# Output stage of a hybrid decoder layer: two kinds of GpSimd sums held at their source place, and a wider spread of one product's weight splits

## The chip, the cores and the metric

One core of a Trainium2 chip runs the whole kernel in one launch. The metric is the device time of an execution in microseconds (us). The engines are TensorE (PE in the profile, with its weight loads as PEld), VectorE (DVE), ScalarE (ACT), GpSimd (POOL) and SyncE (SP), which here only issues DMA transfers.

## What is computed

One decoder layer, for a prompt of 2048 tokens and for 32 sample tokens, in float32. A projection of the normalised input gives four groups of columns: a convolution module, a pooling mixer, a stick-breaking attention and a cross-attention. Each result is multiplied by its gate; the four are concatenated to a row of 2048 and multiplied by `w_out` (2048 x 1024), normalised, added to the input and normalised again. The output stage, on which the change bears, is the last line but one:

```python
mix = jnp.concatenate([y_c * jax.nn.silu(cg), y_p * jax.nn.silu(pg),
                       y_s * jax.nn.silu(sg), y_m * jax.nn.silu(mg)], axis=-1)
out = rms_norm(mix @ w_out, post_g)
return x + out, conv_new, pool_new, k, v
...
y_prompt = rms_norm(xp, final_g)
```

## The kernel before

**The stages.** Input projection and sample attention fill the first 1700 us, prompt attention runs to about 1947 us, and the output stage runs from there to the end, with the last steps of the convolution module (`conv_post`) spread through it.

**The output product in seven.** `mix @ w_out` is cut two by two by two (pairs of token tiles, halves of the 2048, halves of the 1024 columns) and computed from seven block products instead of eight, numbered 1 to 7. Sums and differences of blocks of `mix` and of `w_out` replace the missing product. `weight_sums` made the sums of `w_out` earlier and left them in DRAM (`wsd`). The sums of `mix` are made in this stage by `out_combine`:

- Product 7: POOL subtracts two row blocks (L1702) and SP stores the difference to `msd` for product 6.
- Product 6: DVE subtracts that difference from another block (L1705); the result is the product's own operand. POOL then subtracts it from the rows that product 2 used (L1706), and SP stores this to `msd` (L1617) for product 3. So nothing in product 6 waits for L1706 itself; product 3 does, much later, and SP does at once, since the store stands in its queue.
- Product 5: POOL adds two row blocks (L1699). Both come with the load of product 4 (L1672), so the sum can run as soon as that transfer has landed. Its result is product 5's operand.

**Parts.** A product's work on one pair of token tiles is split into two halves of the contraction. Such a *part* `(product, i, half)` is four quarters, and a quarter is three matmuls against 512 columns: float32 is carried as a rounded high part and a rest, so high times high, rest of the weights times high, high times rest. There are 120 parts in a fixed list: product 1, product 7, then 2 and 6 in alternation, then 4, 5 and 3 in alternation. `i = 8` is the sample tokens. I number parts from 0; part 34 is (2,0,0), parts 38 and 39 are (6,0,0) and (6,0,1), parts 64 to 67 the last of product 6, part 69 is (4,0,1), part 72 the first of product 5.

**What a part needs.** The high and low part of its operand: `out_high`, a cast on ACT (L1714), then `out_low`, a subtraction on DVE (L1725). And four of the eight weight blocks of its product: `weight_high` on ACT (L1621, `wohi`) and `weight_low` on DVE (L1626, `wolo`), from a raw block that SP loads (L1599, L1602 or L1611). The first half of a product uses blocks 0 to 3, the second half blocks 4 to 7, one block per quarter.

**Order.** PE follows the order of the source (`manual_schedule`). On the other engines a planner orders the instructions when the program is built, by its own estimate of when each is ready, and an engine then works its queue strictly in order. So there are two places of an instruction: where the source traces it, and where the planner puts it. `tc.keep_in_program_order(ins)` ties the two a little: `ins` may not be issued ahead of the one instruction that was traced just before it on the same engine. It adds no wait for a result, and later instructions may still go ahead of it. L1621, L1626 and L1705 are held so already.

**Who traces what when.** The main loop walks the parts. After each quarter it advances the convolution by a step whenever a counter, raised by 1 per quarter, passes 0.9 (`OPACE`), then calls `weights_step(n + k / 4)`, which traces the weight steps due by then. `spread(gen, start, step)` makes step `k` of a product's weights due at part `start + step * k`. For product 6 the start is part 31, and block `j` is split in step `3 + j`. At the end of a part, `prepare` loads operands six parts ahead, combines four ahead and casts three ahead. One round of the convolution (`center`, `scale`, `point`) handles 256 tokens: PE sums squares (`cv`, L1460), ACT takes a root (L1461), DVE the reciprocal (L1462), then for two pairs of channel blocks DVE scales (L1469), ACT takes the sigmoid (L1472), DVE multiplies (L1476), ACT casts (L1478), DVE subtracts (L1481); the matmuls `cz` (L1502) of the pointwise layer follow, in four pieces, and DVE empties each from PSUM (L1505). The `cz` pieces share two PSUM buffers.

**Last steps.** `out_factor` (L1788, POOL) multiplies a stored half of the output, `oh`, by a gain, and `out_tile` normalises and stores a token tile. Blocks of `mix` are held in few buffers (`raw`: 4 of two blocks each; `wr`: 2 for weights).

Of the kernel before, what the change touches and what calls it, by code (L numbers as in the profile page):

```python
# [13 lines left out]
ALU = mybir.AluOpType  # L14
# [73 lines left out]
def kernel(  # L88
# [9 lines left out]
    pe, act, dve, pool, sp = nc.tensor, nc.scalar, nc.vector, nc.gpsimd, nc.sync  # L98
# [1492 lines left out]
    def weight_load(prod, j, raw):  # L1591

        if (prod, j) in seconds:
            return [seconds.pop((prod, j))]
        n, h = SUMS.get(prod, (0, 0))
        if raw == "opm":
            t = opm.tile([P, 512], F32, tag="raw", name=f"wor{prod}_{j}", bufs=3)
            if prod in SUMS:
                sp.dma_start(t, wsd[n, j, :, h])  # L1599
            else:  # L1600
                q = FACTORS[prod]
                sp.dma_start(t, w_out0[half_rows(j)[q // 10 - 1], 512 * (q % 10 - 1) : 512 * (q % 10)])  # L1602
            return [t]
        slot = (opx if raw == "wx" else op).tile([P, 2, 512], F32, tag=raw, name=f"wor{prod}_{j}",
                                                 bufs={"raw": RAWS, "wr": 2, "wx": 3}[raw])
        if prod in SUMS:
            two = wsd[n, j : j + 2, :, h]
        else:
            k = 4 + j if j < 4 else j - 4
            two = w_out0.rearrange("(b p) n -> b p n", p=P)[k : k + 2, :, :512]  # L1610
        sp.dma_start(slot, two.rearrange("b p n -> p b n"))  # L1611
        seconds[prod, j + 1] = slot[:, 1]
        return [slot[:, 0]]

    def store(key=None):
        while len(stores) > 2 or key in [k for k, *_ in stores]:
            sp.dma_start(*stores.pop(0)[1:])  # L1617

    def weight_high(prod, j, ts, pool_):
        hi, lo = [pool_.tile([P, 512], F32R, tag=f"wo{n}{j}", name=f"wo{n}{prod}_{j}", bufs=1) for n in ("hi", "lo")]  # L1620
        tc.keep_in_program_order(act.copy(hi, ts[0]))  # L1621
        ts += [hi, lo]

    def weight_low(prod, j, ts, eng):
        raw_, hi, lo = ts
        tc.keep_in_program_order(eng.tensor_tensor(out=lo, in0=raw_, in1=hi.bitcast(F32), op=ALU.subtract))  # L1626
        W[prod, j] = hi, lo

    def out_weights(prod, pool_, eng, lead=1, raw=lambda j: "opm", lag=1):


        ts = {}
        for j in range(lead):
            if j:
                yield
            ts[j] = weight_load(prod, j, raw(j))
        for j in range(8 + lag):
            yield
            if 0 < j < 9:
                weight_high(prod, j - 1, ts[j - 1], pool_)  # L1640
            if j >= lag:
                weight_low(prod, j - lag, ts.pop(j - lag), eng)
            if j < 8:
                store()
            if j + lead < 8:
                ts[j + lead] = weight_load(prod, j + lead, raw(j + lead))
# [47 lines left out]
    def out_combine(x):  # L1694
        prod, i, h = x
        store()
        ts = raws[x]
        if prod == 5 and i < LAST:
            pool.tensor_tensor(out=ts[1], in0=ts[0], in1=ts[1], op=ALU.add)  # L1699
            ts = ts[1:]  # L1700
        elif prod == 7:
            pool.tensor_tensor(out=ts[0], in0=ts[0], in1=ts[1], op=ALU.subtract)  # L1702
            stores.append(((0, i, h), msd[0, i, h], ts[0]))
        elif prod == 6:
            tc.keep_in_program_order(dve.tensor_tensor(out=ts[0], in0=ts[0], in1=ts[1], op=ALU.subtract))  # L1705
            pool.tensor_tensor(out=ts[2], in0=ts[2], in1=ts[0], op=ALU.subtract)  # L1706
            stores.append(((1, i, h), msd[1, i, h], ts[2]))
        raws[x] = ts[0]

# [217 lines left out]
    def side_work():  # L1927
        nonlocal opm, conv
        with tc.tile_pool(name="sm", bufs=1, side="left", reuse_waits="tile") as sm2:
            yield from sample_end(sm2, side_ps, S)  # L1930
        with tc.tile_pool(name="wsp", bufs=1, side="left", reuse_waits="tile") as wsp:
            yield from weight_sums(wsp)
        opm = ox.enter_context(tc.tile_pool(name="opm", bufs=1, side="left", reuse_waits="tile"))
        yield from out_weights(1, opm, pool)
        while (3, 0) not in flags:
            yield
        for x in lead_:
            out_load(x)
            out_combine(x)
            out_high(x)  # L1940
            out_low(x, pool)
            yield

        while (3, 1) not in flags:
            yield
        for x in parts[2 * LEAD : 2 * LEAD + 3]:
            out_load(x)
        cp = cx.enter_context(tc.tile_pool(name="cp", bufs=1, side="left", reuse_waits="tile"))
        conv = conv_post(cp, lambda n: conv_ps[0](n), lambda: cx.enter_context(
            tc.tile_pool(name="cpw", bufs=1, side="left", reuse_waits="tile")))  # L1950
        while "centered" not in flags:
            next(conv)
            yield
# [55 lines left out]
    op = oy.enter_context(tc.tile_pool(name="op", bufs=1, side="right", reuse_waits="tile"))  # L2009
# [9 lines left out]
    def weights_after():  # L2019


        at = parts.index

        def spread(gen, start, step):
            yield start
            for k, _ in enumerate(gen):
                yield start + step * k

        yield 2 * LEAD
        wr = lambda j: "wr"  # L2030
        yield from spread(out_weights(7, op, dve, 2, wr), 2 * LEAD, 1.5)
        yield from spread(out_weights(2, opm, dve, 2, wr), at((7, 0, 0)) + 1, 1.4)

        def place():

            nonlocal op2, opx, accp2
            yield at((2, 7, 0)) - 6
            for _ in conv:
                pass
            cx.close()  # L2040
            accp2 = oy.enter_context(tc.tile_pool(name="ops2", bufs=1, space=PSUM, side="right", reuse_waits="tile"))
            op2 = cx.enter_context(tc.tile_pool(name="op2", bufs=1, side="left", reuse_waits="tile"))
            opx = x6.enter_context(tc.tile_pool(name="opx", bufs=1, side="left", reuse_waits="tile"))

        def fourth():
            yield at((2, 7, 0)) - 5
            yield from spread(out_weights(4, op2, dve, 2, lambda j: "wx"), at((2, 7, 0)) - 4, 1)

        some = ("opm", "wr", "wr", "raw", "raw", "opm", "wr", "wr")
        yield from heapq.merge(spread(out_weights(6, op, dve, 3, lambda j: some[j]), at((2, 0, 0)) - 3, 0.55), place(),  # L2050
                               fourth(), spread(out_weights(5, opm, dve, 2, wr), at((2, 8, 0)) - 1, 1),
                               spread(out_weights(3, op, dve, 2, lambda j: "opm"), last_ + 1, 1))

    wts, wait = weights_after(), 0

    def weights_step(n):
# [11 lines left out]
    def prepare(n):  # L2068
        for d, f in ((3, out_load), (1, out_combine), (0, out_high)):
            for x in parts[: n + d]:  # L2070
                if x in ready[d]:
                    continue
                prod, i, h = x
                if d == 3 and not h and prod == 2:
                    while i < LAST and ("conv", i) not in flags:
                        next(conv, None)
                    if i == LAST:
                        for _ in conv:
                            pass
                f(x)  # L2080
                ready[d].add(x)
# [67 lines left out]
```

## Time and profile before

| | us |
|---|---|
| Runs of the kernel (3): median, lowest, highest | 2359.39, 2356.07, 2364.3 |
| The profiled execution: its own time | 2357.87 |
| Its span, from first to last instruction | 2356.2 |
| PE busy in the span | 2268.6 |
| DVE busy | 1718.0 |
| POOL busy | 1280.6 |
| Last matmul of part 119 begins | 2339 |

All times of the trace are counted from the span's start. The profiled execution lies 1.5 us below the median of the runs. In a row of the timeline stand the start, the time taken, the engine, the line, the operation, what it writes and reads, how many instructions the row merges, and in brackets how long the engine stood idle before it and what ended that. `SPq` is SP's queue: the row's time is the issue of the transfer, not the transfer.

### The profile page before, as it was taken

How to read it: one execution, taken by the hardware profiler on the slowest of the kernel's cores; microseconds unless marked ns; L12 is line 12 of the kernel's file. 1: busy time of each engine (PE TensorE's matmuls, PEld its weight loads, DVE VectorE, ACT ScalarE, POOL GpSimd, SP SyncE). 2: the span in 40 equal slices, each digit the busy share in tenths (PEclk: the TensorE clock that was granted, in tenths of full speed). 3: DMA queues.
4: the chain of work that ended last, by engine and by line, in shares of the span. 5: the costliest groups of instructions: out<-in, count | busy, mean ns of one | idle time of the engine just before them, and what ended most of it. 6: DMA issues, size and time to landing. Idle time of an engine off the chain costs nothing. (4 is left out here: it accounts for less than half of the span.)

```text
span 2356.2 us, 42223 instructions
## 1 busy us (share of the span) xinstructions
PE 2268.6 (96%) x16024; PEld 1767.5 (75%) x16024; DVE 1718.0 (73%) x2428; ACT 1118.3 (47%) x1947; POOL 1280.6 (54%) x1322
## 2 busy tenths in 40 slices
PE   7999999999999999999999999899999999999897
PEld 7998888888888777777777777555555557878775
DVE  5342786969647664577787868888897966787897
ACT  5322343342442322234242324788989875454554
POOL 3554545555464656545546463688988854432330
PEclk9999999999999999999999999999999999999999
DMA  6689977878678899987877884756544207866674
GB/s 212 196 283 298 343 267 257 288 248 289 243 262 314 311 352 338 322 287 260 304 264 257 280 273 143 176 170 165 161 131 117 77 23 225 283 223 215 208 247 159
DMA packets 336870, 557.94 MB, mean 237 GB/s; under 512 B 27986, under 2 KB 212434, under 8 KB 320267
## 3 DMA queue, kind: packets, MB, share of 16 engines
q1 hardware_dynamic: 281290, 286.53, 39.4%
q0 software_dynamic: 55376, 268.72, 32.0%
q8 instruction: 126, 2.06, 0.4%
q14 instruction: 78, 0.63, 0.1%
HBM read 465.09 MB, written 90.68 MB: 236 GB/s over the span
## 5 line engine op out<-in xcount | busy, mean ns | idle before, releaser
L966 DVE STREAM_TRANSPOSE T<-kt 128x1024 f32<-128x1024 f32 x256 | 308.6, 1225 | 182.8 <-PE sSA L979 170.0
L933 POOL DMA_INDIRECT vt<-in_cache_v_dram,idv x256 | 252.8, 988 | 255.5 <-PE sO L1018 194.9
L618 DVE SCALAR_TENSOR_TENSOR cacc<-U,par,cacc 128x512 f32<-128x512 f32 x480 | 359.7, 749 | 11.0
L1344 POOL TENSOR_TENSOR be<-be,E 128x512 f32<-128x512 f32 (+3 forms) x316 | 300.6, 967 | 60.4 <-DVE E L1335 26.6
L1335 DVE TENSOR_TENSOR_SCAN E<-gam,cr,ZM 128x513 f32<-128x513 f32 x192 | 232.7, 1262 | 14.1 <-ACT gam L1266 10.7
L933 POOL DMA_INDIRECT kt<-in_cache_k_dram,idk x128 | 128.3, 1002 | 198.8 <-DVE T L966 157.4
L1355 PEld LDWEIGHTS AT<-ident,be 128*128 128x128 f32 x1082 | 116.1, 141 | 128.0 <-ACT at L1361 48.2
L1969 PE MATMUL acc<-wohi,mh 128*128 128x512 f32 (+1 forms) x480 | 193.5, 403 | 1.9 <-ACT mh L1714 1.9
L1266 ACT ACTIVATE gam<-S,nbias_bc 128x1024 f32<-128x1024 f32 (+1 forms) x158 | 173.1, 1095 | 42.6 <-ACT be L1267 18.5
L1969 PE MATMUL acc<-wolo,mh 128*128 128x512 f32 (+1 forms) x480 | 189.5, 395 | 2.6 <-DVE wolo L1626 2.6
L1969 PE MATMUL acc<-wohi,ml 128*128 128x512 f32 x448 | 177.4, 396 | 5.6 <-DVE ml L1725 5.6
L1262 PE MATMUL S<-kT,Q 128*128 128x512 f32 (+1 forms) x632 | 174.6, 399 | 5.4 <-ACT be L1267 5.4
L1267 ACT ACTIVATE be<-S,bias_bc 128x1024 f32<-128x1024 f32 (+1 forms) x158 | 172.0, 1089 | 1.4 <-DMA gsd<-sg1sg 1.4
L1355 PE MATMUL AT<-ident,be 128*128 128x128 f32 x1082 | 157.3, 283 | 14.0 <-DVE at L1359 7.4
L1371 PE MATMUL av<-at,V 128*64 128x512 f32 (+3 forms) x640 | 152.2, 554 | 3.5 <-DVE sbo L1376 3.5
L979 PE MATMUL sSA<-T,W 128*32 128x128 f32 x4096 | 138.3, 276 | 1.8 <-DVE T L966 1.4
L979 PEld LDWEIGHTS sSA<-T,W 128*32 128x32 f32 x4096 | 104.6, 109 | 36.6 <-issue 29.1
L1018 PE MATMUL sO<-vt,saT 128*32 128x512 f32 x1024 | 122.3, 592 | 0.0
L1725 DVE TENSOR_TENSOR ml<-mr,mh 128x512 fp32r<-128x512 f32 x108 | 95.7, 897 | 35.0 <-ACT mh L1714 33.5
L1262 PEld LDWEIGHTS S<-kT,Q 128*128 128x128 f32 x632 | 105.0, 193 | 19.2 <-ACT be L1267 6.8
L1361 ACT COPY at<-AT 128x512 f32<-128x512 f32 x192 | 111.3, 679 | 12.2 <-PE AT L1355 12.2
L1332 DVE TENSOR_TENSOR_SCAN E<-gam,ZM 128x384 f32<-128x384 f32 (+1 forms) x124 | 94.3, 809 | 28.8 <-ACT gam L1266 22.0
(577 smaller groups left out, 6024.7 us busy)
## 6 DMA issues: line engine op xcount, KB each, us to landing
Q<-qd SPq DMA_DIRECT2D x64, 256.0 KB
mr<-mixd SPq DMA_DIRECT2D x32, 512.0 KB
mr<-mixd SPq DMA_DIRECT2D x48, 256.0 KB
xtp<-in_x_prompt_dram SPq DMA_DIRECT2D x16, 512.0 KB
kT<-kd SPq DMA_DIRECT2D x64, 128.0 KB
ws<-in_w_out_dram SPq DMA_DIRECT2D x16, 512.0 KB
wsd<-ws SPq DMA_DIRECT2D x16, 512.0 KB
msd<-mr SPq DMA_DIRECT2D x32, 256.0 KB
```

The lines of the kernel that those rows point to most:

```text
L618: dve.scalar_tensor_tensor(out=ps, in0=U[:, a + k : a + k + H], scalar=wd[:, k : k + 1], in1=ps, op0=ALU.mult, op1=ALU.add)
L933: pool.indirect_dma_start(out=dst, out_offset=None, in_=rows, in_offset=bass.IndirectOffsetOnAxis(ap=idx, axis=0))
L966: S["turn"] = dve.transpose(T[:, 2 * hh : 2 * hh + 2].rearrange("p s j t -> p (s j t)"), kt[:, 2 * hh : 2 * hh + 2].rearrange("p s j d -> ...
L979: pe.matmul(sSs[n][32 * g : 32 * g + 32, P * ml : P * (ml + 1)], lhsT=W[:, jj, :], rhs=T[:, :, jj, :], start=i == 0, stop=i == 3, tile_pos ...
L1262: pe.matmul(S[:, j, :w], lhsT=Q[:, x, P * (q2 + j) : P * (q2 + j + 1)], rhs=kt[:, :w], start=x == 0, stop=x == 1)
L1266: act.activation(out=ga, in_=S[:, :, :w], func=AF.Sigmoid, bias=nbias_bc[:, h : h + 1], scale=-1.0)
L1267: act.activation(out=be, in_=S[:, :, :w], func=AF.Sigmoid, bias=bias_bc[:, h : h + 1])
L1335: dve.tensor_tensor_scan(out=E[:, j][:, ::-1], data0=g_[:, j][:, ::-1], data1=ZM[:, 0:1].to_broadcast([P, 513]), initial=carry[hh, q2][:, ...
L1344: newest.append(pool.tensor_tensor(out=be[:, j, :m], in0=be[:, j, :m], in1=E[:, j, 513 - w : 513 - w + m], op=ALU.mult).ins)
L1355: pe.transpose(ap_[:, P * qt : P * (qt + 1)], A[hp, qb, kc, hh, qt][:, P * r : P * (r + 1)], ident)
L1371: pe.matmul(av[64 * hh : 64 * hh + 64, c], lhsT=V[:, 4 * kc + r, 64 * hh : 64 * hh + 64], rhs=ats.pop((hp, qb, kc, r, hh))[:, c], start=dg ...
L1969: pe.matmul(o[:rows], lhsT=m[a][:, k, :rows], rhs=W[prod, 4 * h + k][w], start=not cont and h == k == n == 0, stop=h == 1 and k == 3 and n ...
```

## The change

Two calls on POOL, L1699 and L1706, are wrapped in `tc.keep_in_program_order`, as the DVE call beside them already was. And the weight steps of product 6 are due every 0.7 parts instead of every 0.55: block `j` is split at part `31 + 0.7 * (3 + j)`, so block 0 at 33.1 instead of 32.65 and block 7 at 38.0 instead of 36.5. No instruction is added, removed or resized.

```diff
@@ out_combine
         if prod == 5 and i < LAST:
-            pool.tensor_tensor(out=ts[1], in0=ts[0], in1=ts[1], op=ALU.add)
+            tc.keep_in_program_order(pool.tensor_tensor(out=ts[1], in0=ts[0], in1=ts[1], op=ALU.add))
             ts = ts[1:]
...
             tc.keep_in_program_order(dve.tensor_tensor(out=ts[0], in0=ts[0], in1=ts[1], op=ALU.subtract))
-            pool.tensor_tensor(out=ts[2], in0=ts[2], in1=ts[0], op=ALU.subtract)
+            tc.keep_in_program_order(pool.tensor_tensor(out=ts[2], in0=ts[2], in1=ts[0], op=ALU.subtract))
@@ weights_after
-        yield from heapq.merge(spread(out_weights(6, op, dve, 3, lambda j: some[j]), at((2, 0, 0)) - 3, 0.55), place(),
+        yield from heapq.merge(spread(out_weights(6, op, dve, 3, lambda j: some[j]), at((2, 0, 0)) - 3, 0.7), place(),
                                fourth(), spread(out_weights(5, opm, dve, 2, wr), at((2, 8, 0)) - 1, 1),
```

## Prediction

> **What bounds the kernel now.** I read the page first, then the table by stretches (length, busy PE, PEld, DVE, ACT and POOL with counts, TensorE's clock, DMA), then the waits of TensorE in the output stage (total, times, longest), then the timelines around each wait.
>
> ```profile
> span 2356.2 us, 42223 instructions
> PE 2268.6 (96%) x16024; PEld 1767.5 (75%) x16024; DVE 1718.0 (73%) x2428; ACT 1118.3 (47%) x1947; POOL 1280.6 (54%) x1322
> ```
> ```profile
> 2050.00:2100.00 50.00, 45.70 (x231) 38.88 (x230) 43.64 (x73) 26.00 (x53) 16.05 (x15) 0.96 0.71 225
> 2200.00:2250.00 50.00, 47.16 (x205) 37.91 (x204) 44.83 (x77) 26.99 (x67) 8.21 (x6) 1.00 0.68 226
> ```
> ```profile
> PE acc L1969 <- DVE ml L1725: 5.6, 4, 3.5
> PE cz L1502 <- DVE cgt L1505: 4.3, 1, 4.3
> PE cz L1502 <- ACT shi L1478: 2.9, 2, 2.3
> PE acc L1969 <- DVE wolo L1626: 2.6, 1, 2.6
> PE acc L1969 <- ACT mh L1714: 1.9, 2, 1.2
> PE cz L1502 <- DVE slo L1481: 1.2, 2, 0.8
> ```
>
> TensorE is busy 96% of the span, and its order is fixed, so the change can act only through these waits (1930 us to the end): 18.5 us in 12 waits. POOL never ends one directly. DVE is the near second: 43.64 and 44.83 of 50 us. So the gain can hardly pass 18.5 us, and a change that delays one high or low part by more than its slack costs exactly that on the path.
>
> The edits do three things. They have TensorE wait less for `cgt` (term B), they make the last weight block of product 6 late (term C), and they let a POOL difference out sooner (term A).
>
> **Term B: fewer splits ahead of the pointwise layer's emptying.** VectorE and TensorE around the 4.3 us wait:
>
> ```profile
> 2064.87 0.68 DVE L1626 TENSOR_TENSOR wolo<-wor,wohi 128x512 fp32r<-128x512 f32 x1
> ...
> 2072.74 0.69 DVE L1626 TENSOR_TENSOR wolo<-wor,wohi 128x512 fp32r<-128x512 f32 x1
> ...
> 2074.50 4.05 DVE L1626 TENSOR_TENSOR wolo<-wor,wohi 128x512 fp32r<-128x512 f32 x3
> ...
> 2079.61 1.21 DVE L1626 TENSOR_TENSOR wolo<-wor,wohi 128x512 fp32r<-128x512 f32 x1
> 2080.74 0.47 DVE L1505 SCALAR_TENSOR_TENSOR cgt<-cz,par,cgt 128x256 f32<-128x256 f32 x1
> ```
> ```profile
> 2081.26 0.39 PE L1502 MATMUL cz<-shi,pwhi 128*128 128x256 f32 x1 [4.30 <-DVE cgt L1505]
> ```
>
> The third `cz` piece needs the PSUM buffer of the first, and L1505 stands behind a run of L1626. Six of product 6's splits lie before it: one at 2064.87 and the five from 2072.74 to 2079.61. Its own source place is the last quarter of part 35. By the new steps block 4 is due at part 35.9 and block 5 at 36.6, both behind it; four splits stay ahead. So L1505 moves forward by two L1626: 1.21 (row 2079.61) and 4.05 / 3 = 1.35, together 2.6 us. Bounds: 1.2 if the planner moves only one out of the way, 4.3 if the whole wait goes. I take −2.6, since DVE runs without a gap there.
>
> **Term C: the last split of product 6 becomes late.** Block 7's step is due at part 36.5 before and 38.0 after. Because `weight_high` and `weight_low` are held behind the instruction traced just before them, what matters is which one that is. Counting the convolution's steps (one per 0.9 quarter) from the `cv` matmul that the trace shows in the third quarter of part 37, two steps fall into the first quarter of part 38, and they end with the second pair of L1469 and L1472 of that round. Block 7 is traced right behind. So on ACT its cast cannot pass L1472's second pair, and on DVE its subtraction cannot pass L1469's. Now it follows L1505's third piece, far earlier. The round in the trace of before:
>
> ```profile
> 2088.51 0.59 PE L1460 MATMUL cv<-csq,ones_ln 128*128 128x256 f32 x2
> ...
> 2094.96 0.40 PE L1969 MATMUL acc<-wohi,mh 128*128 128x512 f32 x1
> 2095.20 0.39 PE L1969 MATMUL acc<-wolo,mh 128*128 128x512 f32 x1
> ```
> ```profile
> 2089.14 0.45 ACT L1461 ACTIVATE cv<-cv,eps_t 128x256 f32<-128x256 f32 x1 [0.62 <-PE cv L1460]
> ...
> 2098.05 0.84 ACT L1472 ACTIVATE csg<-ct,par 128x256 f32<-128x256 f32 x2 [1.01 <-DVE ct L1469]
> ```
> ```profile
> 2091.05 1.76 DVE L1462 RECIPROCAL cv<-cv 128x256 f32<-128x256 f32 x1
> 2092.71 0.67 DVE L1725 TENSOR_TENSOR ml<-mr,mh 128x512 fp32r<-128x512 f32 x1
> ```
> ```profile
> 2058.60 0.59 PE L1460 MATMUL cv<-csq,ones_ln 128*128 128x256 f32 x2
> ```
> ```profile
> 2069.89 0.84 ACT L1472 ACTIVATE csg<-ct,par 128x256 f32<-128x256 f32 x2 [0.70 <-DVE ct L1469]
> ```
>
> The chain from `cv` (2088.51) to the end of L1472's second pair (2098.89) is 10.4 us. A cast L1621 adds about 0.5 and a split L1626 about 0.7: the low part is there 11.6 us after `cv`. TensorE reaches the fourth quarter of part 39, block 7's first use, at 2094.96 and needs the low part at 2095.20, 6.7 us after `cv`. Both ends hang on the same `cv`, so an earlier or later TensorE does not help: a wait of 11.6 − 6.7 = 4.9 us, where there is none now. Lower bound: L1462 could start at 2089.6 (root done) instead of 2091.05 and the L1725 between could step back, 2.0 less, so 2.9. Upper: block 6's split now falls between L1462 and L1469 (0.7 to 1.2 more), so 6.1. I take +4.9. Behind the waiting cast on ACT stand the squares L1452 and casts L1714; nothing of these is due before TensorE itself moves on. Block 6 is held only behind L1461 and L1462 and comes in time: 2092.8 + 0.7, against its use a quarter ahead of 2094.96.
>
> The weight steps also move their transfers on SP:
>
> ```profile
> 2078.58 0.32 SPq L1681 DMA_DIRECT2D mr<-mixd  x1
> ...
> 2100.43 0.45 SPq L1611 DMA_DIRECT2D wor<-wsd  x1
> ```
>
> The first takes the buffer of blocks 3 and 4 the moment the last of the three L1626 ends, at 2078.55; with block 4 behind L1505's second piece it leaves some 3 us later, for part 41, which starts near 2098 and after term C near 2103: nothing. The second, a weight of product 5, takes the buffer of blocks 6 and 7, free at 2085.9 now and near 2097.5 then: still before 2100.43, nothing. Should either cover fail, the rows behind it on SP are late by the excess.
>
> On TensorE's clock after such a pause: the stretch 2050 to 2100 with the 4.3 us wait shows 0.96, so at most 0.04 × 50 = 2.0 us was withheld; the stretch from 2200, behind a wait of 3.5 us, shows 1.00. I charge nothing and keep 2.0 as the far end. By the Trainium skill, "TensorE: Matmul & The Clock Gate", Part 1, an idle window of about 3.4 us halves the clock until a busy one has passed; worked out from that page, an estimate of 1.7 us more for term C, and the sum below would be +1.6. The trace agrees with it in the first stretch and not in the second.
>
> **Term A: the row sums step behind the last difference of product 6.**
>
> ```profile
> 2185.65 5.03 POOL L1699 TENSOR_TENSOR mr<-mr 128x512 f32<-128x512 f32 x1 [2.81 <-DMA mr<-mixd]
> 2190.63 2.43 POOL L1706 TENSOR_TENSOR mr<-mr,mr 128x512 f32<-128x512 f32 x1
> ```
> ```profile
> 2185.82 0.67 DVE L1705 TENSOR_TENSOR mr<-mr 128x512 f32<-128x512 f32 x1
> ...
> 2189.43 0.67 DVE L1759 TENSOR_TENSOR U<-acc,U 128x512 f32<-128x512 f32 x1
> ...
> 2191.23 0.67 DVE L1725 TENSOR_TENSOR ml<-mr,mh 128x512 fp32r<-128x512 f32 x1
> 2198.28 0.69 DVE L1626 TENSOR_TENSOR wolo<-wor,wohi 128x512 fp32r<-128x512 f32 x1 [6.37 <-ACT wohi L1621]
> ```
> ```profile
> 2193.09 0.33 SPq L1617 DMA_DIRECT2D msd<-mr  x1
> 2193.51 0.39 SPq L1611 DMA_DIRECT2D wor<-wsd  x1
> ```
> ```profile
> 2197.63 0.62 ACT L1621 CAST wohi<-wor 128x512 fp32r<-128x512 f32 x1 [7.80 <-DMA wor<-wsd]
> ```
> ```profile
> 2199.63 0.50 PE L1969 MATMUL acc<-wohi,ml 128*128 128x512 f32 x1 [3.51 <-DVE ml L1725]
> ```
>
> Read backwards: TensorE waits for a low part that DVE has queued behind a split, this waits for the cast, the cast for its weights. Their load left SP at 2193.51, because the store ahead of it waited for the L1706 that ended at 2193.06. That L1706 had its input at 2186.49, but two L1699, ready since their rows had landed, went ahead, the second with 5.03 us where 1.29 is usual (the L1699 further down). With the source place kept, part 67's L1706 precedes every L1699. Best case: 2186.5 + 1.3 = 2187.8, all 5.3 us earlier, and the wait of 3.5 goes. But the L1699 took 5.03 because DVE ran without a gap from 2184 to 2191.9, and L1706 would run into the same stretch: started at 2186.5 it ends near 2190.7, where the L1699 ended, 2.4 us earlier than now. I take −2.4, the row nearest to the case; ends 0 and −3.5.
>
> By the Trainium skill, "SBUF — State Buffer", Who interferes with whom, a DVE instruction with two SBUF inputs and a GpSimd instruction that reads SBUF exclude each other, the one issued second being blocked. The 5.03 us agree. That rule speaks against this term.
>
> The L1699 that step back lose nothing: held behind L1788, the last pair follows
>
> ```profile
> 2299.59 1.29 POOL L1699 TENSOR_TENSOR mr<-mr 128x512 f32<-128x512 f32 x1 [2.29 <-ACT mh L1714]
> 2307.19 1.29 POOL L1788 TENSOR_TENSOR oh<-oh,gpost 128x512 f32<-128x512 f32 x1 [6.31 <-DVE oss L1810]
> ```
> ```profile
> 2328.28 0.39 PE L1969 MATMUL acc<-wohi,mh 128*128 128x512 f32 x1
> ```
>
> and ends about 2311 instead of 2301, for a part that starts at 2328: cast and split (0.6 and 0.7) hide with 15 us left. If that cover were gone, each would cost its lateness on TensorE. The other L1706 already stand behind their predecessors in the planner's queue, but for two neighbouring pairs that are swapped: zero, covered by product 3's distance.
>
> **Sum.** −2.6 + 4.9 − 2.4 = −0.1 us on the profiled execution's 2357.87, so 2357.8; it lies 1.5 under the median of the runs, so 2359.3 there. A measurement of this kernel tells about 0.3%, 7.1 us, from no change.
>
> **Rivals.** (1) *Slower: the late block decides.* Place: fourth quarter of part 39. In the round before, `cv` at 2058.60 to L1472's end at 2070.73 took 12.1 us, 1.7 more than the round that I used; with block 6's split (1.2) term C is 7.8, with the withheld clock 9.8. If the busy DVE that makes this chain long also keeps POOL's difference where it is, A is 0: 9.8 − 2.6 = +7.2, 2366.6. It decides once the chain exceeds 12 us. For: one round shows it. Against: the other shows 10.4.
> (2) *Faster: DVE's backlog goes.* TensorE's pause at part 39 gives DVE time, so C is 2.9, B its whole 4.3, A its whole 3.5, and the `wolo` wait of 2.6 later goes: −7.5, 2351.9. For: all these waits end at DVE. Against: DVE stands idle before 2198.28 for 6.37 us, so its backlog is not carried that far.
> (3) *POOL stays blocked.* The difference ends no earlier, A is 0: +2.3, 2361.7. This is what the port rule named above would do here; for it speaks the 5.03 us, against it that one-input work (L1759, from PSUM) falls between.
> (4) *The change does nothing*, the planner having the same order for other reasons: 2359.4. Against: block 7's place cannot stay.
>
> **How the numbers follow.** Forecast (with 4) 0.43, POOL blocked 0.12, slower 0.27, faster 0.18. The first two lie within 0.3%. Every term at its own end gives −4.3 + 2.9 − 3.5 = −4.9 and −1.2 + 6.1 + 2.0 = +6.9, so 2354.5 to 2366.3; since the planner, whose order the trace does not show, may reorder four engines behind part 31, I reach to both outer rivals: 2351.5 to 2367.5. Faster by over 0.3%: 0.18; within: 0.55; slower: 0.27.
>
> **What would show it.** Right: the 4.3 us wait for `cgt` shrinks to about 2; a new wait of 3 to 6 us of TensorE for `wohi` or `wolo` stands in part 39, with L1621 directly behind L1472's second pair on ACT; near 2190 L1706 precedes the L1699, and the 3.5 us wait for `ml` is about 1. Wrong: no wait in part 39 (then C fails and the kernel is faster by 5), or new waits in products 5 and 3 (then the L1699 lacked their slack).

## The result

| | before | changed |
|---|---|---|
| Median of 13 runs each, us | 2362.53 | 2368.46 |
| Lowest and highest, us | 2356.07 to 2371.92 | 2365.60 to 2377.24 |
| Ratio to before, 95% interval | | 1.0029 (1.0018 to 1.0040) |
| Span of the profiled execution, us | 2356.2 | 2375.5 |
| First matmul of part 18 to the end of the span, us | 356.2 | 364.7 |

By the ratio, the change makes the kernel slower by 6.9 us (4.3 to 9.5); the two medians lie 5.9 us apart. The forecast was no change; the outcome lies near that of rival 1. The two profiled spans differ by far more, 19.3 us, but 10.8 us of this stand ahead of part 18 (its first matmul is at 2000.03 us before and at 2010.81 us after), where every engine does the same work in the same order in both. So the traces are compared from part 18 on.

### The profile page after: what moved, and what is told of

It reads as the page before. It is cut to its first block, busy times and chain, and to the rows that moved or that the text cites. A ratio compares the mean times of both kernels' runs of the same rounds, so it can differ in the third digit from the quotient of the medians.

```text
span 2375.5 us, 42225 instructions
## 1 busy us (share of the span) xinstructions
PE 2279.4 (96%) x16024; PEld 1772.3 (75%) x16024; DVE 1717.0 (72%) x2428; ACT 1117.7 (47%) x1947; POOL 1279.8 (54%) x1322
## 5 line engine op out<-in xcount | busy, mean ns | idle before, releaser
L1725 DVE TENSOR_TENSOR ml<-mr,mh 128x512 fp32r<-128x512 f32 x108 | 94.4, 884 | 38.4 <-ACT mh L1714 38.2
```

## The profile after

The page of the changed kernel, and the waits of TensorE from 1930 us to the end (total, times, longest):

```profile
span 2375.5 us, 42225 instructions
PE 2279.4 (96%) x16024; PEld 1772.3 (75%) x16024; DVE 1717.0 (72%) x2428; ACT 1117.7 (47%) x1947; POOL 1279.8 (54%) x1322
```
```profile
PE acc L1969 <- DVE ml L1725: 7.1, 7, 2.0
PE acc L1969 <- ACT wohi L1621: 5.2, 1, 5.2
PE cz L1502 <- ACT shi L1478: 2.3, 2, 1.7
...
PE acc L1969 <- DVE wolo L1626: 1.5, 2, 0.9
PE cz L1502 <- DVE cgt L1505: 1.0, 1, 1.0
```

Against the table of before, the `cgt` wait has shrunk from 4.3 to 1.0, the longest `ml` wait from 3.5 to 2.0, and a new wait of 5.2 for `wohi` stands alone. The busy times of DVE, ACT and POOL have moved by 1 us at most: no work was added, it only comes at another time.

The new wait, in the timeline of the changed kernel:

```profile
2094.61 2.38 DVE L1725 TENSOR_TENSOR ml<-mr,mh 128x512 fp32r<-128x512 f32 x2
...
2094.76 0.59 PE L1460 MATMUL cv<-csq,ones_ln 128*128 128x256 f32 x2
...
2094.78 0.62 ACT L1714 CAST mh<-mr 128x512 fp32r<-128x512 f32 x1 [3.50 <-DVE mr L1705]
...
2095.41 1.28 ACT L1461 ACT_TABLE_LOAD   x1
...
2096.71 0.45 ACT L1461 ACTIVATE cv<-cv,eps_t 128x256 f32<-128x256 f32 x1
...
2097.45 0.48 DVE L1505 SCALAR_TENSOR_TENSOR cgt<-cz,par,cgt 128x256 f32<-128x256 f32 x1 [0.46 <-DMA cgt<-gcd]
...
2097.85 0.68 DVE L1763 TENSOR_TENSOR c<-acc,U 128x512 f32<-128x512 f32 x1
...
2098.45 0.68 DVE L1705 TENSOR_TENSOR mr<-mr 128x512 f32<-128x512 f32 x1
...
2099.04 1.76 DVE L1462 RECIPROCAL cv<-cv 128x256 f32<-128x256 f32 x1
...
2106.03 0.84 ACT L1472 ACTIVATE csg<-ct,par 128x256 f32<-128x256 f32 x2 [1.07 <-DVE ct L1469]
...
2106.75 0.62 ACT L1621 CAST wohi<-wor 128x512 fp32r<-128x512 f32 x1
...
2107.42 0.79 PE L1969 MATMUL acc<-wohi,mh 128*128 128x512 f32 x1 [5.25 <-ACT wohi L1621]
...
2107.62 0.68 DVE L1626 TENSOR_TENSOR wolo<-wor,wohi 128x512 fp32r<-128x512 f32 x1
...
2108.36 0.79 PE L1969 MATMUL acc<-wolo,mh 128*128 128x512 f32 x1
...
2108.95 0.63 PE L1969 MATMUL acc<-wohi,ml 128*128 128x512 f32 x1
```

Block 7's cast stands directly behind L1472's second pair, as forecast. From `cv` (2094.76) to the end of that pair (2106.87) it is 12.1 us, not the 10.4 that the forecast used. From the start of the reciprocal on, this round takes 7.8 us and that of before took as long (2091.05 to 2098.89). The 1.7 us lie ahead of it, in DVE's queue: the reciprocal starts 4.3 us after `cv`, against 2.5 in the round of before. In both rounds L1763 and L1705 stand directly before it, but here L1763 begins 3.1 us after `cv` instead of 1.3 (2089.84), behind two L1725 and an L1505 that waits for a transfer. ACT's table load now begins only after `cv`, too, but the root was ready at 2097.16, 1.9 us before the reciprocal began. DVE at this place in the kernel before:

```profile
2089.84 0.69 DVE L1763 TENSOR_TENSOR c<-acc,U 128x512 f32<-128x512 f32 x1 [1.02 <-PE acc L1969]
2090.45 0.68 DVE L1705 TENSOR_TENSOR mr<-mr 128x512 f32<-128x512 f32 x1
```

TensorE's matmuls after the wait take 0.79 and then 0.63 where 0.39 is usual. The table by stretches (length, busy times, granted clock, DMA) shows why, for the changed kernel and, in the second fence, for the kernel before, behind its waits of 4.3 and 3.5 us:

```profile
2107.50:2112.50 5.00, 4.86 (x11) 3.48 (x12) 4.08 (x8) 2.27 (x7) 3.93 (x4) 0.50 0.86 265
2215.10:2219.10 4.00, 4.00 (x11) 3.17 (x12) 4.00 (x6) 1.09 (x3) 1.08 (x1) 0.57 0.97 370
```
```profile
2081.26:2085.26 4.00, 4.00 (x17) 3.67 (x18) 4.00 (x7) 1.27 (x3) 1.29 (x1) 0.57 0.72 212
2199.63:2203.63 4.00, 4.00 (x18) 3.31 (x19) 4.00 (x6) 1.16 (x3) 1.09 (x1) 1.00 0.96 362
```

The granted clock was halved for 5 us behind the new wait (0.50). It had been 0.57 behind the wait for `cgt` too, so this wait had cost more than its 4.3 us.

The start of product 4 in the changed kernel:

```profile
2204.53 3.95 POOL L1706 TENSOR_TENSOR mr<-mr,mr 128x512 f32<-128x512 f32 x1 [3.88 <-ACT junk L1729]
...
2208.45 4.91 POOL L1699 TENSOR_TENSOR mr<-mr 128x512 f32<-128x512 f32 x3
2208.51 0.33 SPq L1617 DMA_DIRECT2D msd<-mr  x1
2208.93 0.39 SPq L1611 DMA_DIRECT2D wor<-wsd  x1
```
```profile
2215.10 0.57 PE L1969 MATMUL acc<-wohi,ml 128*128 128x512 f32 x1 [1.88 <-DVE ml L1725]
```

L1706 now precedes the row sums; its store leaves 4.1 us before part 69 begins (2212.61), against 2.4 us in the kernel before. The wait is 1.9 instead of 3.5, but here the clock was 0.57 behind it and had been 1.00 behind the longer one.

## The experiments

Two theories were put against each other first. L: the late eighth block of product 6 is the loss. H: the holds on POOL are.

**The spread alone** (`0.55` to `0.7`, no `keep_in_program_order` added).

> Only the step of 0.7 for product 6's weight splits; both POOL calls without the hold. Theory L (the late eighth block is the cost, and it is larger than forecast): 5 to 7 us slower than before; a wait of TensorE for wohi of about 5 us in part 39, and the first 4 us after it at half the granted clock. The forecast on record (-2.6 + 4.9): 2.3 us slower. Rival H (the holds are the cost): within 2 us of before.

Measured: 1.0034 (1.0020 to 1.0048), 8.0 us slower, 1 us more than theory L said at most. Its DVE and ACT queues have the order of the changed kernel. The waits of TensorE from 2000 us on:

```profile
PE acc L1969 <- ACT wohi L1621: 5.3, 1, 5.3
PE acc L1969 <- DVE wolo L1626: 2.6, 1, 2.6
...
PE cz L1502 <- DVE cgt L1505: 1.0, 1, 1.0
```

The `wohi` wait is there without the holds: theory L.

**The holds alone** (both `keep_in_program_order`, step 0.55), **the row sums alone** (L1699) and **the differences alone** (L1706).

> Only the two holds on POOL (L1699, L1706), step 0.55. Theory L: within 2 us of before; the 4.3 us wait for cgt stays, no wait in part 39. The forecast on record: 2.4 us faster, the wait of 3.5 us for ml at the start of product 4 shrinks to about 1. Rival H: 4 to 7 us slower, with new waits for ml in the last 70 us (products 3 and 5), since the sums step behind the factors L1788.

> Only the hold on the row sums L1699. Theory L: within 1 us of before. Rival H: carries the loss, 3 to 5 us slower, with waits for ml of 0.3 to 1 us each in the last 70 us, after a POOL queue in which each L1699 stands behind an L1788.

> Only the hold on the differences L1706. The forecast on record: 2.4 us faster if this hold is what puts the last difference of product 6 ahead of the row sums. Theory L: the store leaves about 1.7 us earlier, as in the changed kernel, and the ml wait at the start of product 4 is 1.5 us shorter, but TensorE's clock then halves for some 4 us: within 1 us of before. Rival H: within 1 us of before as well, unless the differences themselves cost, then 2 us slower with a wait of 2 us for ml in part 48.

Measured: 1.0018 (1.0006 to 1.0031), 1.0010 (0.9996 to 1.0023) and 1.0010 (0.9999 to 1.0022), so 4.3, 2.4 and 2.4 us slower, the last two not certainly. The holds are not free either: L's "within 2 us" is missed, and 4.3 us lies in the range of H. But the two losses do not add: 8.0 and 4.3 us alone are 6.9 together. It is the hold on the *sums*, not that on the differences, that puts part 67's L1706 ahead of both of the first L1699; with the differences held one sum still precedes it. In the trace with the sums held the wait for `ml` at part 69 falls from 3.5 to 0.55 us (the stretch from part 69 to part 70 is 3.0 us shorter). What it costs is seen 80 us later. POOL and DVE in the kernel with the sums held, and then in the kernel before at the same place:

```profile
2268.47 1.77 POOL L1788 TENSOR_TENSOR oh<-oh,gpost 128x512 f32<-128x512 f32 x1 [10.32 <-DVE acc L1769]
...
2270.20 3.42 POOL L1699 TENSOR_TENSOR mr<-mr 128x512 f32<-128x512 f32 x2
...
2272.59 2.12 DVE L1815 SCALAR_TENSOR_TENSOR oxt<-oxt,oss,gfin 128x1024 f32<-128x1024 f32 x1
2273.59 2.27 POOL L1788 TENSOR_TENSOR oh<-oh,gpost 128x512 f32<-128x512 f32 x1
2274.75 1.13 DVE L1798 TENSOR_TENSOR oss<-ssk 32x1 f32<-32x1 f32 x1
...
2275.82 3.13 POOL L1699 TENSOR_TENSOR mr<-mr 128x512 f32<-128x512 f32 x2
```
```profile
2269.49 1.28 DVE L1815 SCALAR_TENSOR_TENSOR oxt<-oxt,oss,gfin 128x1024 f32<-128x1024 f32 x1
2270.81 0.15 DVE L1798 TENSOR_TENSOR oss<-ssk 32x1 f32<-32x1 f32 x1
...
2272.50 1.53 POOL L1699 TENSOR_TENSOR mr<-mr 128x512 f32<-128x512 f32 x1 [3.66 <-DMA mr<-mixd]
...
2279.22 1.91 POOL L1699 TENSOR_TENSOR mr<-mr 128x512 f32<-128x512 f32 x1 [5.19 <-DMA mr<-mixd]
```

Held behind L1788, which waits 10.32 us for DVE, two pairs of sums run with two L1788 as one lump of 10.5 us on POOL. Beside it L1815 takes 2.12 instead of 1.28 and L1798, one column of 32 rows, 1.13 instead of 0.15: DVE loses 1.8 us, and an `ml` that it makes then is late.

**The last blocks early** and **the last block free.** The eighth block is taken out of the round in two ways: by a ceiling on the due time, which also brings the seventh forward by 0.2 parts, or by leaving the eighth block's two instructions out of the hold.

```diff
-        def spread(gen, start, step):
+        def spread(gen, start, step, most=1000):
...
-                yield start + step * k
+                yield start + min(step * k, most)
...
-  spread(out_weights(6, ...), at((2, 0, 0)) - 3, 0.55)
+  spread(out_weights(6, ...), at((2, 0, 0)) - 3, 0.7, 6.1)
```

> Step 0.7 for product 6's splits, but blocks 6 and 7 due at part 37.1 at the latest, so ahead of the convolution round in part 37; no holds on POOL. Theory L (the eighth block behind that round is the loss of the spread): the wait for wohi in part 39 and the halved clock behind it go, 8.4 us less than the spread alone; the shorter wait for cgt in part 36 stays (4.7 us gained). So between 4 us faster than before and the same. Rival D (the spread loses by moving the DVE and SP queues as a whole, the block is only where it shows): at least 3 us slower than before, the wait shifting to another operand between parts 38 and 49.

```diff
-        tc.keep_in_program_order(act.copy(hi, ts[0]))
+        (tc.keep_in_program_order if (prod, j) != (6, 7) else id)(act.copy(hi, ts[0]))
```

> Step 0.7 as in the change, but block 7 of product 6 alone is not held (its cast L1621 and subtraction L1626 may go ahead of what was traced before them); no holds on POOL. Theory L with the hold as its cause: the planner takes block 7 out of the round, the wait for wohi in part 39 goes, and the time is 4 us faster than before to the same. If the place is set by the operands and not by the hold: the wait of 5 us stays, 6 to 8 us slower. Rival D: at least 3 us slower.

(The second does the same to L1626.) Measured: 1.0002 (0.9992 to 1.0013) and 0.9992 (0.9979 to 1.0004). The wait for `wohi` is in neither trace, and the 8.0 us that the spread alone had lost are gone: the cause is block 7's place, and the place is the work of the hold. Not all of it comes back as gain with the blocks early, because the next wait shows: in part 41 TensorE then waits for `shi` (1.2) and `slo` (1.0) of the convolution round itself, and the stretch from part 38 to part 42 keeps 2.8 of its 8.4 us.

**Only the cast free**, the subtraction still held.

> Step 0.7; of block 7 of product 6 only the cast L1621 on ACT is free, the subtraction L1626 on DVE stays held behind the second pair of L1469. Theory L (both engines tie the block to the round): the wait of 5.3 us for wohi in part 39 becomes one of 3.5 to 4.5 us for wolo, and the time is that of the spread alone less 1 to 2 us. If the cast alone ties it: no wait over 1 us in part 39, 7 to 8 us less than the spread alone.

```profile
2096.65 0.87 DVE L1469 SCALAR_TENSOR_TENSOR ct<-cy,par,cv 128x256 f32<-128x256 f32 x2
2097.43 0.68 DVE L1626 TENSOR_TENSOR wolo<-wor,wohi 128x512 fp32r<-128x512 f32 x1
```
```profile
2098.17 0.79 PE L1969 MATMUL acc<-wolo,mh 128*128 128x512 f32 x1 [4.57 <-DVE wolo L1626]
```

The high part is early, the low part stays tied behind L1469's second pair, and the wait is 4.6 instead of 5.3. So the tie on DVE is enough by itself for most of the wait. With both tied TensorE waits for the cast, so ACT ties the block as well; a kernel with the tie on ACT alone was not run. From part 18 to the end this one takes 1.5 us less than the spread alone; its one run, 2367.76, tells no more.

**Only the first two sums held**, and **only the later ones**, from (5,3,0) on.

```diff
-            pool.tensor_tensor(out=ts[1], in0=ts[0], in1=ts[1], op=ALU.add)
+            (tc.keep_in_program_order if i == 0 else id)(pool.tensor_tensor(out=ts[1], in0=ts[0], in1=ts[1], op=ALU.add))
```

> Step 0.55; only the first two of the row sums L1699, those of (5,0,0) and (5,0,1), are held, nothing else. On POOL this moves one instruction: the last difference of product 6 goes ahead of these two sums. Theory S (the later sums, lumped behind L1788 in a busy stretch of VectorE, lose what the first two gain): 2.5 us faster than before, the ml wait of 3.5 us at the start of product 4 down to 1, and none of the new waits for ml of the last 60 us. Rival F (the loss of the held sums is not theirs but differs from execution to execution): the same as with all sums held, 0 to 2.4 us slower than before.

> Step 0.55; the row sums L1699 of product 5 held from (5,3,0) on, the first six free. On POOL each later pair of sums now follows an L1788, as with all sums held; the last difference of product 6 stays behind two sums as before. Theory S (the lump of L1788 and two or four L1699 takes VectorE's time): 3 to 5 us slower than before, a wait for ml of about 1 us in part 97, and the ml wait of 3.5 us at the start of product 4 stays. Theory F: within 1 us of before.

(The later ones: `if i > 2`.) Measured: 0.9997 (0.9983 to 1.0011) and 1.0002 (0.9987 to 1.0016). With the first two held the wait at part 69 falls to 0.9:

```profile
2206.02 0.50 PE L1969 MATMUL acc<-wohi,ml 128*128 128x512 f32 x1 [0.89 <-DVE ml L1725]
```

Theory S had said 2.5 us faster and 3 to 5 us slower. The times don't tell S from F: 0.7 us faster and 0.5 us slower are not clear of zero, with intervals of 3 us to either side. The traces do in part. In part 97 all four kernels with the later sums held lose 1.1 to 1.4 us against the kernel before, the nine others at most 0.4. From part 104 to the end the four lie 1.1 to 1.6 us above the second profile of before, the others from 2.1 below to 0.8 above it, on average level with it. So the lump costs 1.1 to 1.4 us in part 97. From part 104 on it may cost as much again, but there two profiles of the kernel before differ by more. The measured times neither bear this out nor exclude it.

**The kernel before once more.**

> The kernel before, unchanged, for a second profile of it. The first profiled execution showed no wait of TensorE after 2236 us. If that was an execution with little lost (theory F): this profile shows waits for ml of 0.2 to 0.7 us each in the last 60 us, 1.5 to 3 us from part 104 to the end more than the first. If those waits belong to the changed orders: none here either, within 0.5 us.

Its two longest waits of TensorE from 2000 us on are those of the first profile:

```profile
PE acc L1969 <- DVE ml L1725: 5.1, 3, 3.5
PE cz L1502 <- DVE cgt L1505: 4.3, 1, 4.3
```

From part 104 to the end it needed 2.07 us more than the first, with the same program and the same order on every engine. That is the time that F had said for this profile. The prediction was summed on an execution that had lost less at its end than most; its base was low too (2359.39 as the median of 3 runs, 2362.53 of 13).

**Both repairs together.** First the early blocks with the first two sums held, then the free block with the same.

> Step 0.7 with blocks 6 and 7 due at part 37.1 at the latest, and only the first two row sums L1699 held. Theories L and S together: the two gains add, 2.5 to 6 us faster than before. Rivals D and F: slower than before by 2 us or more.

> Step 0.7 with block 7 of product 6 not held, and of the row sums only those of (5,0,0) and (5,0,1) held. The two single runs gave -1.9 and -0.7 us against before, and their traces -4 in part 36 and -2.6 at the start of product 4. If the two add: 2 to 6 us faster than before. If the shorter wait at the start of product 4 is given back in product 5 or 3: within 2 us of the kernel with block 7 alone freed.

Measured: 1.0001 (0.9980 to 1.0022), where 2.5 to 6 us faster was expected, but its runs reach from 2351.77 to 2373.23, so undecided; and 0.9981 (0.9970 to 0.9993), 4.5 us faster than before (1.7 to 7.1). The second beats both kernels. In its trace the gains of part 36 and of part 69 both stand.

## Why the prediction was wrong, by its steps

The differences of the stretches between first matmuls of parts, in us, against the second profile of before. The last row is the measured time against before.

| Parts | before, first | changed | spread alone | holds alone | sums held | block free, first sums |
|---|---|---|---|---|---|---|
| 18 to 36 | +0.4 | +0.7 | +1.5 | +0.2 | +0.1 | +0.2 |
| 36 to 38 (term B) | 0.0 | −4.8 | −4.8 | 0.0 | −0.2 | −4.8 |
| 38 to 42 (term C) | 0.0 | +9.1 | +8.4 | 0.0 | 0.0 | +1.6 |
| 42 to 69 | +0.5 | +2.3 | 0.0 | +2.9 | +2.7 | +1.0 |
| 69 to 70 (term A) | 0.0 | −0.1 | +2.0 | −2.6 | −3.0 | −3.0 |
| 70 to 82 | −1.0 | −3.2 | +0.1 | −0.4 | +0.5 | +0.4 |
| 82 to 104 | 0.0 | +1.3 | 0.0 | +1.3 | +2.3 | +1.9 |
| 104 to the end | −2.1 | +1.1 | +0.1 | +1.3 | +1.6 | +0.5 |
| sum | −2.2 | +6.3 | +7.3 | +2.6 | +4.1 | −2.3 |
| measured | | +6.9 | +8.0 | +4.3 | +2.4 | −4.5 |

Not every row is the change's. Between part 42 and part 50, and between 80 and 82, kernels whose queues agree there differ by up to 4 us. The +2.7 of the sums held is of this kind: it lies before part 50, and there all queues of that kernel have the order of before. Of the 4.3 us of the holds alone the traces therefore place only a part. Rows B and C are steady: 0.2 us at most among four kernels with the old step, except 0.5 and 0.7 in row B of the two kernels not shown with the differences or the later sums held. In the changed kernel C comes out 4.2 us above the forecast, B 2.2 below it and A 2.3 above it; the stretches from part 82 on add 2.4 us that it had at nothing, some of which may be the execution's own.

- **Term C, the failed step.** The mechanism and the place were right: block 7's cast behind L1472, a wait in the fourth quarter of part 39. Its size was +4.9 and is +9.1 (8.4 with the spread alone). The waits there sum to 5.9 us (0.54, 5.25 and 0.14), inside the bounds of 2.9 to 6.1; the chain was 12.1 us, as in the slower of the two rounds, and part of that came back since TensorE needed the block 7.4 us after `cv`, not 6.5. Of the other 3.2 us, 2.8 are the halved clock: 0.50 from the end of the wait at 2107.42 to 2112.98, half of 5.6 us. On it the forecast put nothing, with a far end of 2.0. The last 0.4 us are not placed.
- **Term B** was forecast at −2.6 and is −4.8: 3.3 us of waiting, since two splits did go behind L1505, and 1.5 more. For these stands the clock behind the old wait, 0.50 from 2081.76 to 2085.17, half of 3.4 us. (Of the six splits that the prediction counts, the first is a row at 2068.70; that at 2064.87 is still product 2's. The count holds.) The forecast read 0.96 over 50 us as at most 2.0 us and then left it out; a window set behind the wait itself would have shown 0.57.
- So the clock was left out of both terms. Measured, B + C is +4.3, not +2.3.
  By the Trainium skill, "TensorE: Matmul & The Clock Gate", Part 1, an idle window of about 3.4 us brings the clock down to half, and the window runs freely. The forecast gave the estimate of 1.7 us from this page and went by the one row that seemed to speak against it (1.00 behind 3.5 us). The halving behind 5.25 us agrees with the page, since there TensorE was idle for the whole of 2102.75 to 2106.16; that behind 1.88 us, with 1.53 of 3.41 us busy, does not follow from it. The last section shows what decided between 0.50 and 1.00.
- **Term A** was forecast at −2.4 on TensorE, and is −2.6 to −3.0 where the sums are held with the old step. L1706 took 3.95 us in the dense stretch, as the bound from the 5.03 us row said, so rival 3 did not come true in its sense: POOL was blocked for as long, but the store still left earlier. In the changed kernel the wait shrank only to 1.9, and the clock halved behind it took the gain back (−0.1). Against the spread alone, whose wait of 4.0 us was followed by a halved clock as well, it shows (+2.0 to −0.1).
- **The sums stepping back "lose nothing"**: this was wrong in kind. Their deadline was met, as forecast. What the step did not price is the time that they take from DVE when they run in a lump. The Trainium skill, "SBUF — State Buffer", Who interferes with whom, says that a DVE instruction with two SBUF inputs and a GpSimd instruction that reads SBUF exclude each other; L1798's 1.13 us agree (both its inputs lie in SBUF). The forecast used that rule for one instruction of POOL and not for the ten that it moved.
- **The rivals.** Rival 1 happened nearly as written: the chain beyond 12 us, the withheld clock, A without a net gain; it said +7.2, and +6.9 was measured. It had 0.27. That the sums are so near is partly luck: C was 9.1 and not 9.8, B −4.8 and not −2.6, POOL's difference did come earlier, and the stretches from part 82 on, where rival 1 had nothing, took 2.4 us more. Rival 2 is out: in the spread alone, with the same pause of TensorE at part 39, the waits of 4.0 us for `ml` and of 2.6 for `wolo` stayed. Rival 4 is out by the order of block 7. What speaks for a higher chance of rival 1 was in the trace of before already: of the two rounds that it showed, one had the 12.1 us.

Open is the wait of 2.0 us for `ml` in part 48 of the changed kernel. The spread alone and the second profile of before lose nothing more there than the first, five other kernels lose 0.6 to 1.2, some of them with the queues of before there, and two gain 0.7; no run separates the cause.

## What to carry to other kernels

Before a step is moved in the source under a hold, ask which instruction will then stand just ahead of it on that engine, and when this one ends in the *slowest* round that the trace shows; a wait of several microseconds on TensorE is then to be priced with the clock behind it, read in a window of 4 us that begins where the wait ends: here 1.5 us behind 4.3 us of waiting, and 2.8 behind 5.25. Hold only the instructions that have to give way, not all of their kind: the two first sums gave the whole gain at part 69, and holding the others only crowded VectorE later. And an instruction that meets its deadline can still cost, if it runs beside a busy engine that it blocks.

## What the runs showed of the hardware that was not expected

The same wait is followed by different clocks. Behind 3.4 to 3.5 us at the start of product 4 the clock was 1.00 in both profiles of before, and 0.50 in the kernel with the later sums held (the first row is of the second profile of before, the other of the kernel with the later sums held):

```profile
2208.45:2212.45 4.00, 4.00 (x18) 3.29 (x18) 4.00 (x6) 1.23 (x4) 1.08 (x1) 1.00 0.99 370
```
```profile
2209.00:2213.00 4.00, 4.00 (x11) 3.13 (x10) 3.83 (x7) 1.99 (x4) 0.00 (x0) 0.50 1.04 407
```

That is 18 matmuls in 4 us against 11, and 2 us of the path, with the same work on either side.

What decides is where the wait lies. In each of the fourteen profiles, from 1955 us to shortly before the end, the halved stretches are one or two steps of 3.41 us long and all begin on one raster of such steps, whose place differs from execution to execution. In 38 of these steps TensorE was busy for less than 0.44 of the time, and the next step was halved every time. After a step at full clock with TensorE busy for over 0.64 it never was, and between the two either happened. The steps around the two waits, of the first profile of before and of the kernel with the later sums held:

```profile
2194.40:2197.81 3.41, 1.71 (x8) 1.09 (x6) 0.00 (x0) 0.18 (x1) 0.00 (x0) 1.00 0.97 314
2197.81:2201.22 3.41, 1.59 (x7) 1.34 (x8) 2.94 (x4) 1.99 (x4) 1.62 (x1) 1.00 0.92 292
```
```profile
2203.27:2206.68 3.41, 1.17 (x6) 0.63 (x4) 0.17 (x1) 0.82 (x2) 0.00 (x0) 1.00 1.07 320
2206.68:2210.09 3.41, 2.23 (x5) 1.82 (x6) 3.24 (x4) 1.35 (x3) 1.63 (x1) 0.50 0.95 281
```

In the first, 3.51 us of waiting fall half into one step and half into the next, TensorE is busy for 1.71 and 1.59 of 3.41 us, and the clock stays. In the second, most of 3.42 us falls into one step, 1.17 us are busy, and the next two steps are halved. Of the six waits of 3.4 to 3.6 us at this place, four were followed by a halved clock; the wait of 4.3 us for `cgt` was in all seven profiles that have it. So behind a wait of 3.5 us a forecast should carry both values, and behind one of over 4 us the halved one.

And the time that one execution needs up to part 18 varied by 14.9 us (1997.2 to 2012.1) among profiles of programs that are alike up to there, while the output stage of the same kernel varied by 2.2 us (356.2 and 358.4). For an effect of a few microseconds the stage's own span says more than the whole time.
